# Row-by-row first projections, squares added on VectorE, a later row of factors, and sums at the end on TensorE

## The chip, the cores and the metric

The kernel runs on one core of one Trainium2 chip. A core has a matrix engine (TensorE, PE in the profile), VectorE (DVE), ScalarE (ACT), GpSimd (POOL) and SyncE (SP), which here issues the transfers. The metric is the device time of one execution in microseconds (us).

## The reference

256 tokens of width 1024 pass through two blocks in fp32. The first has attention and a mixture of 32 experts. The second is where most of the change lies: four feed-forward stages of width 2816 (ffn0 to ffn3), with a mixer with forgetting attention (fox) behind the first and one with latent attention (mla) behind the third. Each stage begins with a norm over the width.

```python
def rms_norm_2(x, g):
    xf = x.astype(jnp.float32)
    y = xf * lax.rsqrt(jnp.mean(xf * xf, axis=-1, keepdims=True) + RMS_EPS)
    return (y * g.astype(jnp.float32)).astype(x.dtype)

def swiglu(x, w_gate, w_up, w_down):
    return (jax.nn.silu(x @ w_gate) * (x @ w_up)) @ w_down
...
    for layer in range(DEPTH_2):
        h = h + 0.5 * swiglu(rms_norm_2(h, norm_ffn[layer, 0]), ffn_w_gate[layer, 0],
                             ffn_w_up[layer, 0], ffn_w_down[layer, 0])
        hn = rms_norm_2(h, norm_mix[layer])
...
            h = h + pool_fox_mixer(hn, ab_w_in[i], ab_b_forget[i], pool_w[i], pool_scale[i], ab_w_out[i])
...
            h = h + mla_mixer(hn, cos, sin, mla_w_in[i], mla_q_norm[i], mla_kv_norm[i],
...
        h = h + 0.5 * swiglu(rms_norm_2(h, norm_ffn[layer, 1]), ffn_w_gate[layer, 1],
                             ffn_w_up[layer, 1], ffn_w_down[layer, 1])
    return rms_norm_2(h, norm_final)
```

## The kernel before

The stream of activations lies transposed in SBUF (`xT`): 8 rows (`j`, or `kk` where they are contracted) of 128 channels by 256 tokens. A product keeps fp32 accuracy by splitting both sides into a high and a low half: ACT writes the high half (L195 for weights, L199 for activations), DVE subtracts it to get the low half (L196, L200), and `mm` (L149) does three matmuls for each 128 x 128 block: high by high, high by low, low by high (`ws`). Weights come from HBM through SP into `raw` tiles and are split into `hl` tiles, half a tile in each instruction.

A feed-forward stage (`ffn`) goes through 11 chunks of 256 inner columns. A chunk has three projections of 48 matmuls each: gate (into a PSUM tile `ps`), up (`psq`) and down (`psa`); down of a chunk runs behind up of the next one. `ws` first does all 8 rows for the chunk's first 128 columns (a column block), then all 8 for the second.

The norm is not applied ahead of the projections. `prep` splits `xT` with the gains alone, and squares it on the side: ACT squares two rows, `squares` adds them up (L251) and halves the sum (L253). `add_sums` sums it over channels on PE with a column of ones, `rstd` (L234, L218) and `rsqrt_of` (L219 to L229, three Newton steps of four instructions on POOL, of three on DVE) take the inverse root, and `row` spreads it over the partitions: two diagonals (`dg`, L270) by a matrix of ones on PE, copied by DVE (L273). `act` multiplies gate and up by that row of factors (L1150, L1152). So a stage's gate needs only the splits, and the factors are needed when the first chunk is activated; `aH` and `aL` are the halves of the activated chunk, which down reads.

ffn0 has its own `prep_first`, with two norms in one. Its `xT` comes from the last experts: `spread` adds the experts' results to `xT` (L982). At the end `finish` is called by the last down for each row: it squares and sums for the last norm, and `turn` transposes back to tokens by channels.

Each engine runs its instructions in the order that a scheduler of the framework gives them by its own estimates; `issue_after` only says what an instruction must stand behind, and `pins` are the last splits of a stage.

## Time and profile before

| what | value |
|---|---|
| timed runs | 1662.88, 1662.97, 1671.75 us, median 1662.97 |
| profiled execution | 1667.76 us, span 1666.0 |
| mean granted clock of TensorE | 0.977 of full |
| busy | PE 95%, weight loads 75%, DVE 56%, ACT 35%, POOL 11% |
| chain that ended last | PE 52%, DVE 5%, DMA 2%, others 1% or less each |

The span runs from the first to the last instruction; the execution's own time also counts what lies around it. By the traces' times ffn0 takes from about 690 to 885 us, fox to 988, ffn1 to 1175, ffn2 to 1368, mla to 1464, ffn3 to 1653. A busy engine in a timeline row is one that has instructions under way; the bracket at a row's end gives the idle time just before it and what ended it.

### The profile page before, as it was taken

The numbers are of one execution on the slowest core, as the hardware profiler recorded it, in microseconds if no ns is written. First come the engines' busy times: TensorE is split into PE (matmuls) and PEld (weight loads), VectorE is DVE, ScalarE is ACT, GpSimd is POOL, SyncE is SP. The second block draws the span as 40 slices with busy tenths as digits, with TensorE's granted clock in tenths as the row PEclk, the third lists the DMA queues.
The fourth block names the chain that finished last, engine by engine and source line by source line (L and its number), as shares of the span: only waits on it lengthen the run. The fifth ranks groups of instructions, "written<-read, shape, count | busy, mean of one in ns | idle before, by whom it ended". The sixth has DMA issues, their size and how long they took to land.

```text
span 1666.0 us, 26914 instructions
## 1 busy us (share of the span) xinstructions
PE 1579.0 (95%) x11231; PEld 1247.7 (75%) x11231; DVE 927.6 (56%) x1645; ACT 579.0 (35%) x885; POOL 184.0 (11%) x296
## 2 busy tenths in 40 slices
...
GB/s 379 307 207 136 264 364 366 411 421 420 421 421 421 421 421 416 351 217 205 186 181 156 123 99 193 197 200 191 164 182 195 180 155 120 71 180 200 196 108 26
DMA packets 62252, 411.11 MB, mean 247 GB/s; under 512 B 6704, under 2 KB 8752, under 8 KB 15920
## 3 DMA queue, kind: packets, MB, share of 16 engines
...
## 4 chain that ended last, share of the span: by engine, by line
PE 52%; DVE 5%; DMA 2%; POOL 1%; issue 1%; ACT 1%; DVEq 0%; SPq 0%; POOLq 0%; ACTq 0%
PE psa L149 20%; PE ps L149 17%; PE psq L149 15%; DVE x L200 1%; DVE hl L196 1%; DMA we<-in_we_dram 1%; DMA hl<-in_we_dram 1%; PE psa L448 1%; DVE xT L1141 0%; POOL rt L226 0%; POOL dg L270 0%; ACT hl L195 0%; POOL rt L227 0%; POOL ry L219 0%; POOL ry L229 0%
## 5 line engine op out<-in xcount | busy, mean ns | idle before, releaser
L195 ACT ACTIVATE hl<-raw 128x1024 fp32r<-128x1024 f32 (+1 forms) x338 | 346.6, 1060 | 414.2 <-issue 249.0
L196 DVE TENSOR_TENSOR hl<-raw,hl 128x1024 fp32r<-128x1024 f32 (+1 forms) x336 | 412.0, 1244 | 121.6 <-ACT hl L195 121.2
L149 PE MATMUL ps<-x,hl 128*128 128x256 f32 x3120 | 400.4, 287 | 14.1 <-DVE x L200 9.6
L149 PEld LDWEIGHTS ps<-x,hl 128*128 128x128 f32 x3120 | 381.1, 193 | 31.4 <-DVE x L200 12.6
L149 PE MATMUL psq<-x,hl 128*128 128x256 f32 x2160 | 259.1, 279 | 0.0
L149 PEld LDWEIGHTS psq<-x,hl 128*128 128x128 f32 x2160 | 253.7, 189 | 0.0
L149 PE MATMUL psa<-aH,hl 128*128 128x256 f32 x1408 | 251.5, 279 | 0.0
L149 PEld LDWEIGHTS psa<-aH,hl 128*128 128x128 f32 x1408 | 217.2, 188 | 0.3 <-DVE xT L1137 0.3
L149 PE MATMUL psa<-aL,hl 128*128 128x256 f32 x704 | 196.3, 279 | 0.0
L149 PEld LDWEIGHTS psa<-aL,hl 128*128 128x128 f32 x704 | 133.0, 189 | 0.0
L149 PE MATMUL psa<-hl,XT 128*64 128x512 f32 x464 | 120.8, 599 | 1.4 <-DMA hl<-in_we_dram 1.4
L1029 ACT ACTIVATE ym<-psa,gs 128x512 fp32r<-128x512 f32 x32 | 21.9, 687 | 249.0 <-PE psa L149 244.2
L149 PE MATMUL psa<-raw,XT 128*64 128x512 f32 x368 | 100.4, 599 | 1.4 <-DVEq L851 1.1
L982 DVE SCALAR_TENSOR_TENSOR xT<-ps,mod,xT 128x256 f32<-128x256 f32 x128 | 55.6, 479 | 77.9 <-PE ps L149 77.6
L251 POOL TENSOR_TENSOR sq<-sq,sq 128x512 f32<-128x512 f32 x18 | 26.8, 1491 | 464.3 <-ACT sq L244 460.7
L149 PEld LDWEIGHTS psa<-hl,XT 128*64 128x64 f32 x464 | 34.9, 137 | 55.9 <-issue 48.1
L1150 DVE TENSOR_TENSOR gr<-ps,row 128x512 f32<-128x512 f32 x44 | 30.4, 690 | 77.8 <-PE ps L149 77.8
L1030 DVE SCALAR_TENSOR_TENSOR ym<-psa,gs,ym 128x512 fp32r<-128x512 f32 x32 | 24.0, 750 | 88.4 <-ACT ym L1029 86.7
L149 PEld LDWEIGHTS ps<-GT,ym 128*128 128x128 f32 x256 | 34.2, 189 | 50.2 <-issue 38.3
L1152 DVE TENSOR_TENSOR ur<-psq,row 128x512 f32<-128x512 f32 x44 | 30.4, 690 | 74.0 <-PE psq L149 74.0
L1007 ACT ACTIVATE ac<-psa 128x512 f32<-128x512 f32 x16 | 9.6, 597 | 166.9 <-PE psa L149 140.4
L149 PE MATMUL psa<-hl,aT 128*64 128x512 f32 x240 | 63.9, 619 | 0.3 <-DVE aT L1019 0.2
...
## 6 DMA issues: line engine op xcount, KB each, us to landing
...
hl<-in_we_dram SPq DMA_DIRECT2D x88, 1024.0 KB, 18.5
...
```

Source lines behind the costliest of these rows:

```text
L149: return getattr(PE.matmul(o, l, r, start=start, stop=stop, **kw), "ins", None)
L195: A.activation(H[:, c:c + n], src[:, c:c + n], AF.Copy)
L196: (late[c > 0] if late else V).tensor_tensor(L[:, c:c + n], src[:, c:c + n], H[:, c:c + n].bitcast(F32), op=OP.subtract)
L200: v = V.scalar_tensor_tensor(L, src, scale, H.bitcast(F32), op0=OP.mult, op1=OP.subtract)
L251: E.tensor_tensor(acc[:, :w], acc[:, :w], sq[:, :w], op=OP.add)
L448: PE.transpose(bk[:, n * 128:(n + 1) * 128], P[:, n * 128:(n + 1) * 128], ident)
L982: V.scalar_tensor_tensor(xT[:, j, :], po[:, (j % 2) * T:(j % 2 + 1) * T], g2c[:, j:j + 1], xT[:, j, :], op0=OP.mult, op1=OP.add)
L1007: A.activation(ac, p1, AF.Silu)
L1029: last = A.activation(H, py[n], AF.Copy, scale=gs).ins
L1030: V.scalar_tensor_tensor(L, py[n], gs, H.bitcast(F32), op0=OP.mult, op1=OP.subtract)
L1150: V.tensor_tensor(gr, v2(pg), b2(r), op=OP.mult)
L1152: V.tensor_tensor(ur, v2(pu), b2(r), op=OP.mult)
```

## The change

1. `ws_by_k` takes the place of the first projection of each stage: for each row `kk` it goes over both column blocks, six matmuls, before the next row. It is used for chunk 0's gate, for the first projection of fox and for the first of mla.
2. The adds of squares of `prep` and `prep_first` are issued behind all eight splits, and on DVE instead of POOL.
3. In ffn1 to ffn3 the row of factors comes behind chunk 1's gate, as it did in ffn0, and chunk 0's activation with it. In ffn0 the weights of chunk 1's up wait for the end of the inverse root on DVE (`ended`) rather than for a shift (`shifted`).
4. ffn0's splits are issued in pairs between the four spreads of the last experts.
5. At the end rows 4 to 7 are squared on ACT and summed by PE alone; DVE multiplies the first half of the channels by the norm's gains straight from PSUM (before: an ACT copy and a POOL product); two of the four stores are issued by ACT.

```diff
@@ -210,7 +210,7 @@
     def small2(tag, dt=F32, w=2):
         return sm_p.tile([128, w], dt, tag=f"{tag}{w}", name=nm(tag), bufs=2 if w == 2 else 1)
-    shifted = []
+    shifted, ended = [], []
     def rsqrt_of(v, E=None, w=2):
         E = G if E is None else E
@@ -221,7 +221,7 @@
             if E is V:
                 V.scalar_tensor_tensor(t, y, -0.5, y, op0=OP.mult, op1=OP.mult)
                 V.tensor_tensor(t, t, v, op=OP.mult)
-                V.scalar_tensor_tensor(y, t, 1.5, y, op0=OP.add, op1=OP.mult)
+                ended[:] = [V.scalar_tensor_tensor(y, t, 1.5, y, op0=OP.add, op1=OP.mult).ins]
             else:
                 G.tensor_tensor(t, y, y, op=OP.mult)
                 G.tensor_tensor(t, t, v, op=OP.mult)
@@ -291,6 +291,17 @@
             mm(po, h, XH[:, k0 + kk, :], start and kk == 0, False, **kw)
             mm(po, h, XL[:, k0 + kk, :], False, False, **kw)
             i = mm(po, l, XH[:, k0 + kk, :], False, stop and kk == nk - 1, **kw)
+        return i
+
+    def ws_by_k(po, HL, XHL):
+
+        (H, L), (XH, XL) = HL, XHL
+        for kk in range(KD):
+            for m in range(2):
+                pm_, c = po[:, m * T:(m + 1) * T], slice(m * 128, m * 128 + 128)
+                mm(pm_, H[:, kk, c], XH[:, kk, :], kk + m == 0, False, skip_group_check=True)
+                mm(pm_, H[:, kk, c], XL[:, kk, :], False, False, skip_group_check=True)
+                i = mm(pm_, L[:, kk, c], XH[:, kk, :], False, kk == KD - 1, skip_group_check=True)
         return i
     def xs(po, HL, XHL, t0, c0, n, nk=KD, k0=0, start=True, stop=True):
@@ -1031,6 +1042,7 @@
         pin.append(last)
         due.extend(lambda b=b: spread(y, GT, b) for b in range(4))
+    pins, first_x = [], []
     XT, part = gather(chosen(0))
     part(0, 4)
     for p in range(NEXP // 2):
@@ -1042,7 +1054,7 @@
         W = nextW
         if part:
             XT = nextXT
-        if p in (13, NEXP // 2 - 1):
+        if p == 13:
             while due:
                 due.pop(0)()
         if p == 4:
@@ -1050,11 +1062,15 @@
         if p == 13:
             overflow()
+    first_x += [x8(F32R), x8(F32R)]
+    for b in range(4):
+        due.pop(0)()
+        for j in (2 * b, 2 * b + 1):
+            pins[:] = split(xT[:, j, :], first_x[0][:, j, :], first_x[1][:, j, :], scale=gg[:, j:j + 1])
+
     pm.close()
     pe.close()
     mark("second")
-
-    pins = []
     def after(pins):
         es = ExitStack()
@@ -1067,8 +1083,8 @@
         acc = None
         for j in range(KD):
             pins[:] = split(xT[:, j, :], XH[:, j, :], XL[:, j, :], scale=col(gname, g0 + j))
-            if j % 2:
-                acc = squares([xT[:, j - 1:j + 1, :]], acc=acc, halve=j == KD - 1)[0]
+        for j in range(1, KD, 2):
+            acc = squares([xT[:, j - 1:j + 1, :]], acc=acc, eng=V, halve=j == KD - 1)[0]
         if raw_sums:
             return (XH, XL), acc
@@ -1082,15 +1098,13 @@
         return (XH, XL), narrow
     def prep_first(pool):
-        XH, XL = x8(F32R), x8(F32R)
-        for j in range(KD):
-            pins[:] = split(xT[:, j, :], XH[:, j, :], XL[:, j, :], scale=gg[:, j:j + 1])
+        XH, XL = first_x
         w = small2("rw")
         def narrow(behind):
             bank = psa()
             v = small2("rv")
-            acc2 = squares(halves(xT), scale="fg", halve=True)[0]
+            acc2 = squares(halves(xT), scale="fg", eng=V, halve=True)[0]
             acc1 = squares(halves(xT), first=pool.tile([128, 2, T], F32, name="acc1"), eng=V, halve=True)[0]
             with tc.issue_after(behind):
                 add_sums(bank, 0, acc2)
@@ -1177,13 +1191,13 @@
                 if c == 0:
                     HLu = wf(1, c, KD)
             pg = ps()
-            last = project(HLg, pg)
-            if c == 1 and not n:
+            last = project(HLg, pg) if c else ws_by_k(pg, HLg, XHL)
+            if c == 1:
                 with tc.issue_after(last):
                     r = row(*rn)
                 act(*held, r)
             if c:
-                with tc.issue_after(shifted[-1]) if c == 1 else ExitStack():
+                with tc.issue_after(shifted[-1] if n else ended[0]) if c == 1 else ExitStack():
                     HLu = wf(1, c, KD)
             elif n:
                 rn = narrow(last)
@@ -1193,11 +1207,8 @@
                 rn = narrow(last)
             if not c:
                 acc4 += [psa() for _ in range(4)]
-                if not n:
-                    held = (c, pg, pu)
-                    continue
-                with tc.issue_after(last):
-                    r = row(*rn)
+                held = (c, pg, pu)
+                continue
             act(c, pg, pu, r)
         down(*prev.pop())
         pfs.close()
@@ -1228,7 +1239,7 @@
     u = wx.tile([128, 4, 16 + T], F32, name="uf")
     V.memset(u[:, :, 0:16], 0.0)
     pu = [ps(), psq()]
-    last = proj2(abload(0), pu[0])
+    last = ws_by_k(pu[0], abload(0), XHL)
     rt, bank = narrow(last)
     last = proj2(abload(1), pu[1])
     pf = ps()
@@ -1380,7 +1391,7 @@
     pkv, pq = psa(), ps()
     sums = psa()
-    last = proj2(miload(1), pkv)
+    last = ws_by_k(pkv, miload(1), XHL)
     kvHL, sq = latent(pkv, 1, "kvn", "ckv")
     with behind(last):
         add_sums(sums, 0, acc)
@@ -1480,29 +1491,28 @@
             for i in range(2):
                 PE.transpose(bank[2 * i + j // 4][:, (j % 4) * 128:(j % 4 + 1) * 128], xT[:, j, i * 128:(i + 1) * 128], ident)
-    def gain():
-        for i in range(2):
-            o = po_.tile([128, 512], F32, name=nm("o"))
-            A.activation(o, bank[2 * i], AF.Copy)
-            G.tensor_tensor(o, o, nfb[:, 0:512], op=OP.mult)
-            gained.append(o)
+    def gain(i):
+        o = po_.tile([128, 512], F32, name=nm("o"))
+        V.tensor_tensor(o, bank[2 * i], nfb[:, 0:512], op=OP.mult)
+        gained.append(o)
     def finish(j):
         if j == 1:
             bank.extend([ps(), ps(), psq(), psq(), psa()])
-        if j < 6:
-            acc[:] = squares([xT[:, j - 1:j + 1, :]], acc=acc[0] if acc else None, eng=V, halve=j == 5)
+        if j < 4:
+            acc[:] = squares([xT[:, j - 1:j + 1, :]], acc=acc[0] if acc else None, eng=V, halve=j == 3)
             turn(range(j - 3, j - 1) if j > 1 else [])
-        else:
-            if j == 6:
-                turn([4, 5])
-                gain()
-                add_sums(bank[4], 0, acc[0])
-            sq = po_.tile([128, 1, T], F32, name=nm("sq"))
-            A.activation(sq[:, 0], xT[:, j], AF.Square)
-            add_sums(bank[4], 0, sq, False)
-        if j == 7:
-            turn([6, 7])
+            return
+        first = j - 1 if j == 5 else j
+        if j == 5:
+            add_sums(bank[4], 0, acc[0])
+        sq = po_.tile([128, j + 1 - first, T], F32, name=nm("sq"))
+        A.activation(sq, xT[:, first:j + 1], AF.Square)
+        for q in range(j + 1 - first):
+            add_sums(bank[4], 0, sq[:, q:q + 1], False)
+        turn({5: [2, 3], 6: [4, 5], 7: [6, 7]}[j])
+        if j > 5:
+            gain(j - 6)
     ffn(3, 24, finish)
@@ -1513,8 +1523,8 @@
         A.activation(gained[i], gained[i], AF.Copy, scale=r[:, i:i + 1])
         o = po_.tile([128, 512], F32, name=nm("o"))
         V.scalar_tensor_tensor(o, bank[2 * i + 1], r[:, i:i + 1], nfb[:, 512:], op0=OP.mult, op1=OP.mult)
-        for q, t in enumerate((gained[i], o)):
-            SP.dma_start(out[i * 128:(i + 1) * 128, q * 512:(q + 1) * 512], t)
+        for q, (t, E) in enumerate(((gained[i], A), (o, SP))):
+            E.dma_start(out[i * 128:(i + 1) * 128, q * 512:(q + 1) * 512], t)
 def lay_out(i):
```

DVE at the start of ffn2, before: the end of the splits of `xT` (`x_1441` is the low half), the weight splits (`hl`), the variance (`rv`) and its shift (`ri`), up to the row of factors.

```order
L200 SCALAR_TENSOR_TENSOR x_1441_10316<-xT,cols,x_1440_10315 128x256 x4
L196 TENSOR_TENSOR hl_10505<-raw_10502,hl_10504 128x1024 x2
L196 TENSOR_TENSOR hl_10513<-raw_10510,hl_10512 128x1024 x2
L234 TENSOR_SCALAR rv_10413<-psa_10410 128x2
L218 TENSOR_SCALAR ri_10415<-rv_10413 128x2
L196 TENSOR_TENSOR hl_10570<-raw_10567,hl_10569 128x1024 x2
L273 COPY row_10490<-psa_10410 128x256
```

The same place in the changed kernel:

```order
L251 TENSOR_TENSOR sq_10333<-sq_10333,sq_10335 128x512
L196 TENSOR_TENSOR hl_10488<-raw_10485,hl_10487 128x1024
L251 TENSOR_TENSOR sq_10333<-sq_10333,sq_10338 128x512
L196 TENSOR_TENSOR hl_10488<-raw_10485,hl_10487 128x1024
L251 TENSOR_TENSOR sq_10333<-sq_10333,sq_10341 128x512
L196 TENSOR_TENSOR hl_10562<-raw_10559,hl_10561 128x1024
L253 TENSOR_TENSOR sq_10333<-sq_10333 128x256
L196 TENSOR_TENSOR hl_10562<-raw_10559,hl_10561 128x1024
L234 TENSOR_SCALAR rv_10413<-psa_10410 128x2
L218 TENSOR_SCALAR ri_10415<-rv_10413 128x2
L196 TENSOR_TENSOR hl_10570<-raw_10567,hl_10569 128x1024 x2
L196 TENSOR_TENSOR hl_10685<-raw_10682,hl_10684 128x1024 x2
```

The row just ahead of these is the last four activation splits (L200), and the row's copy comes next behind them. The three adds and the halving now stand between the weight splits, ahead of `rv`. Between `ri` and the row's copy stood two weight splits and now stand four.

PE in ffn2, before, around the diagonals: the last rows of chunk 0's up (`psq`), and chunk 1's gate (`ps`).

```order
L149 MATMUL psq_10432<-x_1440_10315,hl_10355 128x256
L149 MATMUL psq_10432<-x_1441_10316,hl_10355 128x256
L149 MATMUL psq_10432<-x_1440_10315,hl_10356 128x256
L149 MATMUL psa_10410<-dg_10485,cstt 128x128 x2
L149 MATMUL ps_10518<-x_1440_10315,hl_10512 128x256
L149 MATMUL ps_10518<-x_1441_10316,hl_10512 128x256
```

The changed kernel, around the diagonals:

```order
L149 MATMUL ps_10493<-x_1440_10315,hl_10487 128x256
L149 MATMUL ps_10493<-x_1441_10316,hl_10487 128x256
L149 MATMUL ps_10493<-x_1440_10315,hl_10488 128x256
L149 MATMUL psa_10410<-dg_10542,cstt 128x128 x2
L149 MATMUL psq_10575<-x_1440_10315,hl_10569 128x256
L149 MATMUL psq_10575<-x_1441_10316,hl_10569 128x256
```

The diagonals now stand behind chunk 1's gate and ahead of chunk 1's up; chunk 1's gate moved ahead of them.

DVE at the end of the program, before: the last evacuations of ffn3 into `xT`, the squares, and the variance of the last norm.

```order
L1141 SCALAR_TENSOR_TENSOR xT<-psa_13607,xT 128x512
L1141 SCALAR_TENSOR_TENSOR xT<-psa_13608,xT 128x512
L251 TENSOR_TENSOR sq_15454<-sq_15454,sq_15469 128x512
L1141 SCALAR_TENSOR_TENSOR xT<-psa_13609,xT 128x512
L1137 SCALAR_TENSOR_TENSOR xT<-psa_13610,xT 128x256
L251 TENSOR_TENSOR sq_15454<-sq_15454,sq_15489 128x512
L253 TENSOR_TENSOR sq_15454<-sq_15454 128x256
L1137 SCALAR_TENSOR_TENSOR xT<-psa_13610,xT 128x256
L234 TENSOR_SCALAR rv_15536<-psa_15453 128x2
```

The changed kernel, same place (`o` are the products with the gains):

```order
L1155 SCALAR_TENSOR_TENSOR xT<-psa_13607,xT 128x512
L1155 SCALAR_TENSOR_TENSOR xT<-psa_13608,xT 128x512
L251 TENSOR_TENSOR sq_15454<-sq_15454,sq_15469 128x512
L1155 SCALAR_TENSOR_TENSOR xT<-psa_13609,xT 128x512
L253 TENSOR_TENSOR sq_15454<-sq_15454 128x256
L1496 TENSOR_TENSOR o_15517<-ps_15449,x_1765_13433 128x512
L1151 SCALAR_TENSOR_TENSOR xT<-psa_13610,xT 128x256
L1496 TENSOR_TENSOR o_15534<-psq_15451,x_1765_13433 128x512
L1151 SCALAR_TENSOR_TENSOR xT<-psa_13610,xT 128x256
L234 TENSOR_SCALAR rv_15537<-psa_15453 128x2
```

One add of squares is gone, the halving stands ahead of the last two evacuations instead of between them, and two products from PSUM are new.

## Rows read from the trace of the kernel before

**Rows 1.** The page, part 1: busy us by engine (share of span).
```profile
PE 1579.0 (95%) x11231; PEld 1247.7 (75%) x11231; DVE 927.6 (56%) x1645; ACT 579.0 (35%) x885; POOL 184.0 (11%) x296
```

**Rows 2.** PE's waits, whole span: what for, us in total, times, longest.
```profile
PE ps L149 <- DVE x L200: 9.6, 13, 2.2
...
PE psa L149 <- POOL dg L270: 6.7, 5, 2.2
```

**Rows 3.** Timeline of PE, start of ffn2: start, us, instruction, count, idle before.
```profile
1175.63 1.64 PE L149 MATMUL ps<-x,hl 128*128 128x256 f32 x13
...
1180.29 5.29 PE L149 MATMUL ps<-x,hl 128*128 128x256 f32 x29 [0.80 <-DVE x L200]
1185.42 0.50 PE L149 MATMUL psa<-cstt,sq 128*128 128x1 f32 x4
...
1192.30 0.84 PE L149 MATMUL psa<-dg,cstt 128*128 128x128 f32 x4 [0.62 <-POOL dg L270]
...
1198.63 1.58 PE L149 MATMUL psq<-x,hl 128*128 128x256 f32 x12
```

**Rows 4.** Timeline of DVE, start of ffn2.
```profile
1173.03 0.48 DVE L200 SCALAR_TENSOR_TENSOR x<-xT,cols,x 128x256 fp32r<-128x256 f32 x1 [0.58 <-ACT x L199]
...
1176.47 4.63 DVE L200 SCALAR_TENSOR_TENSOR x<-xT,cols,x 128x256 fp32r<-128x256 f32 x4
1181.03 4.62 DVE L196 TENSOR_TENSOR hl<-raw,hl 128x1024 fp32r<-128x1024 f32 x4
...
1198.47 0.69 DVE L196 TENSOR_TENSOR aL<-gr,aH 128x512 fp32r<-128x512 f32 x1 [0.70 <-ACT aH L195]
```

**Rows 5.** Timeline of POOL, start of ffn2.
```profile
1175.66 4.30 POOL L251 TENSOR_TENSOR sq<-sq,sq 128x512 f32<-128x512 f32 x3 [170.70 <-ACT sq L244]
...
1186.68 1.19 POOL L226 TENSOR_TENSOR rt<-ry 128x2 f32<-128x2 f32 x1
...
1189.65 0.19 POOL L226 TENSOR_TENSOR rt<-ry 128x2 f32<-128x2 f32 x1
...
1191.88 0.72 POOL L270 TENSOR_SCALAR dg<-cstt,ry 128x128 f32<-128x128 f32 x2
```

**Rows 6.** Windows: us, busy us by engine, granted PE clock (PEclk), DMA share, GB/s.
```profile
1001.00:1013.00 12.00, 10.04 (x72) 9.78 (x72) 5.58 (x9) 3.70 (x5) 2.94 (x14) 0.86 0.59 223
1172.00:1190.00 18.00, 16.21 (x122) 15.46 (x121) 15.76 (x20) 9.70 (x17) 8.03 (x11) 0.91 0.40 148
```

**Rows 7.** Timeline of PE, start of ffn1.
```profile
988.98 2.32 PE L149 MATMUL ps<-x,hl 128*128 128x256 f32 x19
...
1012.44 1.75 PE L149 MATMUL psq<-x,hl 128*128 128x256 f32 x14
```

**Rows 8.** Timeline of PE, start of ffn3.
```profile
1464.16 0.28 PE L149 MATMUL ps<-x,hl 128*128 128x256 f32 x1
...
1487.68 2.54 PE L149 MATMUL psq<-x,hl 128*128 128x256 f32 x21
```

**Rows 9.** Timeline of PE, start of fox.
```profile
905.99 0.84 PE L149 MATMUL psa<-dg,cstt 128*128 128x128 f32 x4 [0.86 <-POOL dg L270]
```

**Rows 10.** Timeline of DVE, start of mla.
```profile
1381.54 0.17 DVE L218 TENSOR_SCALAR ri<-rv 128x4 int32<-128x4 int32 x1
```

**Rows 11.** Timeline of DVE, end of the program.
```profile
1649.82 0.69 DVE L251 TENSOR_TENSOR sq<-sq,sq 128x512 f32<-128x512 f32 x1 [0.77 <-ACT sq L244]
...
1653.09 1.37 DVE L253 TENSOR_TENSOR sq<-sq 128x256 f32<-128x256 f32 x1
...
1657.49 0.16 DVE L234 TENSOR_SCALAR rv<-psa 128x2 f32<-128x2 f32 x1 [2.70 <-PE psa L149]
```

**Rows 12.** Timeline of SP's queue, end of the program.
```profile
1660.65 1.81 SPq L1517 DMA_DIRECT2D out_dram<-o  x4
```

**Rows 13.** Chain that ended last, two projections of 48, ffn0 and ffn1.
```profile
744.79 5.65 PE ps L149 x48
...
1018.04 5.44 PE psa L149 x48
```

## The prediction

> **What bounds the kernel now.** I read the page first. TensorE (PE) is busy for 1579.0 of the 1666.0 us of the span [rows 1], so only what stops PE, or slows it, can be gained. The list of PE's waits comes next, since it says what ends those stops. Two of its entries belong to code that the change touches: 13 waits for the low half of a split activation row (`x`, L200, DVE), 9.6 us together and 2.2 the longest, and 5 waits for the factors' diagonal (`dg`, L270, POOL), 6.7 us [rows 2]. They lie at the starts of the six stages behind the experts: ffn0, fox, ffn1, ffn2, mla, ffn3.
>
> The timeline of one such start shows how it goes. In ffn2 the gate begins at 1175.63 and the matmuls of the sums follow at 1185.42 [rows 3]. That is 9.79 us for 48 matmuls, which take 5.65 at the slower of two paces that PE keeps (48 in 5.65 or in 5.44, 117.8 or 113.3 ns each [rows 13]). 4.1 us are lost. DVE and POOL show why: a split that runs alone takes 0.48, the last four take 4.63 together, 1.16 each [rows 4], while POOL adds squares (three in 4.30 [rows 5]). The old gate spends three matmuls on a split, 0.35 us, and so waits 0.80 for the next. The windows show the rest: PE's granted clock is 0.91 of full in 1172 to 1190 and 0.86 in 1001 to 1013 [rows 6], that is a stretch at 1.2 instead of 2.4 GHz that costs about 0.09 x 18 = 1.6 and 0.14 x 12 = 1.7 us. In ffn2 it comes straight behind these waits: the 29 matmuls from 1180.29 take 5.1 us until the sums, where 3.4 would do [rows 3].
>
> **The change, part by part.** I work out ffn2 and carry it to the others.
>
> *Row by row over both blocks (`ws_by_k`).* A split now feeds six matmuls, 0.71 us at 117.8 ns. Alone it costs DVE 0.48, so PE should no longer wait.
>
> *Squares on DVE.* The order puts them behind the eight splits, between splits of weights. An add alone costs 0.69 on DVE [rows 11], so three and the halving (half as wide, from that estimated at 0.4) cost 2.5. What they leave is 4 x (1.16 - 0.48) = 2.7, the time that the splits lost to POOL's adds. DVE's own total stays the same, but the activation is ready 2.7 us sooner. The sums are ready later relative to the gate: splits done at 1176.5 + 1.9 = 1178.4, then three adds, three weight splits (1.16 each [rows 4]) and the halving, 6.0 us, so 1184.4. The order has PE reach the sums 19 matmuls into the up projection, at 1175.6 + 67 x 0.1178 = 1183.5. That is a new wait of 0.9; I take 1.0.
>
> *Row held a projection longer.* Before, the diagonal's matmuls stood behind up(0) and waited for POOL until 1192.30, with up(1) at 1198.63 [rows 3]. Now gate(1) stands between: three projections of 48 (17.0), the sums 0.5, the wait 1.0 and the diagonal 0.7 (1198.63 - 1192.30 less 48 matmuls) [rows 3] give up(1) at 1175.6 + 19.2 = 1194.8, 3.8 sooner. The diagonal is due 0.7 earlier, at 1194.1. Behind it stands down(0), which needs `aL`: that ended 6.9 after the diagonal's matmuls started (1198.47 + 0.69 - 1192.30 [rows 3, 4]), while down(0) now follows their start by 0.7 + 5.65 = 6.35 and spends four matmuls, 0.5, on `aH` first: nothing, or with a weight split in the way up to 1.2; I take 0.2. ffn2: **+3.6** (2 to 4.5).
>
> *ffn1.* The gate starts at 988.98, up(1) at 1012.44 [rows 7]. Three projections at 113.3 ns (16.3), sums 0.5, a wait of 0.3 (the order has one of its adds among the splits already) and 0.7 for the diagonal put up(1) at 1006.8: 5.6 sooner, less 0.4 for `aL`, which comes later here against the faster pace. **+5.2** (3.5 to 6). *ffn3* starts at 1464.16, up(1) at 1487.68 [rows 8]: 16.3 + 0.5 + 1.0 + 0.7 = 18.5, so 1482.7, 5.0 sooner, less 0.8 (the same, and a weight split). **+4.2** (2.5 to 5).
>
> *fox* keeps its diagonal where it was, behind the first projections, at 905.99 [rows 9]. The gate ends some 4 us sooner, but the diagonal hangs on the sums, the inverse root on POOL and weight splits on DVE, all of which the adds now delay. I take a third of it, **+1.6** (0.5 to 3). *mla* waits for four factors of which the last is ready at 1381.54 [rows 10], behind weight splits on DVE that do not move: **0** (-0.5 to 2). *ffn0* has the longest of the split waits, 2.2 [rows 2], but its gate's bank is one that the spreads use, and their evacuations now stand among the splits, so it starts no sooner; what goes are the pauses behind. **+1.5** (0 to 3, the longest wait and a little more).
>
> *End.* Before, DVE's last evacuation stood behind a halving that POOL stretched to 1.37 (from 1653.09), and the variance came at 1657.49 [rows 11]. After it the chain is PE's sums, evacuated variance, ten small DVE steps, two products, the store. Now that halving is gone from there and POOL does nothing. Replaying with 0.69 for each of the two products that DVE takes over, its last evacuation starts at about 1653.3 and the variance at about 1655.2: 2.2 sooner. SP issued four stores in 1.81 [rows 12]; it now issues two, the last 0.4 to 0.9 sooner if ACT's take no longer than SP's, an issue that no row shows; I take 0.5. **+2.7** (1 to 4).
>
> The new wait for the sums may itself bring a stretch at the lower clock at one of the starts, as the waits before did (1.6 [rows 6]); with that and what the diagonal may cost in the rival below I take off 1.0. Everything else is covered: a stage that starts 4 to 6 us sooner asks for its weights sooner, and ACT and DVE, 35 and 56% busy [rows 1], have the room to split them.
>
> **Sum.** 1.5 + 1.6 + 5.2 + 3.6 + 0 + 4.2 + 2.7 - 1.0 = 17.8 us, between 8 and 26 with all bounds at their ends. The profiled execution took 1667.76 (its span 1666.0), 4.8 above the median of 1662.97; the timed runs reach from 1662.88 to 1671.75. So 1667.8 - 17.8 = **1650.0**. I don't shift it by 4.8: the likely cause of that spread is the next point, and it is drawn anew.
>
> **Rivals.**
> 1. *The pace.* ffn0 runs at 5.65 for 48, ffn1 at 5.44 [rows 13]; ffn2 is like the first and ffn3 like the second. Each is held through some 1500 matmuls, so it is worth 31 x 0.21 = 6.5 us in a stage. The clock is full in both, and the pace changes only where PE is disturbed. I found no rule in it and count each as the toss of a coin, expected no change. With three of four slow the time would be 1656.5, with all four 1663: no change that a measurement shows.
> 2. *The diagonal is late after all.* POOL's inverse root has 13 short steps; those that meet a weight split on DVE take up to 1.19 instead of 0.19 [rows 5]; in ffn2 two did. The order now has four weight splits between the shift (`ri`) and the row's copy, in ffn1 five. Two more hits put `dg` at about 1185.4 + 3.6 + 4 x 0.9 + 0.7 = 1193.3, and it is due at 1194.1: just in time. Three hits more and each FFN waits some 1.9: 1655.7. The Trainium skill (SBUF — State Buffer, "Who interferes with whom") says that DVE instructions with two SBUF inputs and GpSimd instructions that read SBUF exclude each other, the later one waiting until the first is done. By it every split behind `ri` can hold a step of POOL for its whole length, which is this rival; the trace agrees, with 1.19 against 0.19 [rows 5].
> 3. *The clock stays.* If the stretches at 1.2 GHz come anyway (another pause ahead of them), 5 of the 17.8 don't come: 1655.
> 4. *DVE becomes the bound: slower.* Each start's 2.5 us of adds stand ahead of the weight splits that PE needs next. If PE waited for all 2.5 at the six starts and each wait brought a stretch of 1.7 at the lower clock, that is 25 us: 1650 + 25 = 1675. It ends slower from about 3.6 per start on. For it: DVE is busy without a pause there. Against: DVE gets back the 2.7 it lost to POOL, and PE has a projection of 5.5 us in hand before the next weights.
>
> **How the numbers follow.** No change is what lies within 0.5% (8.3 us) of 1663, so faster is below 1654.7 and slower above 1671.3. Forecast 0.64; the diagonal 0.12, half of it mild enough to stay below 1654.7; the pace 0.12; the clock 0.06; DVE 0.06. Faster 0.64 + 0.06 = 0.70, the same 0.06 + 0.12 + 0.06 = 0.24, slower 0.06. The forecast's own range is 1641 to 1658. For 8 in 10 the upper end takes in the diagonal and most of the pace, 1662; the lower end is the sum with its gains near their upper bounds or one slow stage turned fast, 1639.
>
> **What would show it.** Right: the waits for `x` gone from the starts of ffn1, ffn2 and ffn3, up(1) 4 to 6 us sooner after the stage's first matmul, a wait of about 1 for the sums on DVE, none for `dg` in these stages, full clock in 1172 to 1190, the variance of the end some 2 sooner. Wrong: waits for `hl` or `dg` of several us there, or more stages at 5.65 than before.

## The result, and the profile after

The changed kernel has a median of 1655.95 us against 1663.81 for the kernel before on the same chip (nine executions each; two of the changed one were disturbed, at 2746 and 3949 us, and are left out of the ratio). The ratio is 0.9935, interval 0.9911 to 0.9959: faster by 0.65%. That is also the ratio of the means, 1653.97 and 1664.85; by the medians it is 0.47%. The prediction drew its line for no change at 0.5%, and this line lies inside the interval: that the kernel is faster is shown, that it is so by more than 0.5% is not. The forecast was 1650.0 in 1639 to 1662. The profiled execution took 1654.91 us, span 1653.1, 12.9 below that of before.

The page's first part and the list of PE's waits of the changed kernel, for [rows 1, 2]:

```profile
PE 1577.7 (95%) x11239; PEld 1248.5 (76%) x11239; DVE 926.0 (56%) x1670; ACT 579.2 (35%) x883; POOL 158.3 (10%) x270
```

```profile
PE psa L149 <- POOL dg L270: 5.1, 3, 3.1
PE ps L149 <- DVE xT L993: 4.0, 3, 2.5
```

The wait for `x` (L200), 9.6 us before, is not in the list any more. The one for `xT` (the spreads at ffn0's start) has grown from 1.5 to 4.0, and the halved squares now cost 0.5 in ffn2 and 0.3 in fox. The wait for the diagonal has fallen from 6.7 to 5.1, and it has moved: in ffn1 to ffn3, where it was 2.0, 0.6 and 2.2, none is left, and 3.1 of it is in ffn0.

Timeline of PE, start of ffn2, for [rows 3]:

```profile
1169.14 5.60 PE L149 MATMUL ps<-x,hl 128*128 128x256 f32 x48
1174.58 2.32 PE L149 MATMUL psq<-x,hl 128*128 128x256 f32 x19
1177.41 0.58 PE L149 MATMUL psa<-cstt,sq 128*128 128x1 f32 x4 [0.52 <-DVE sq L253]
...
1181.23 5.60 PE L149 MATMUL ps<-x,hl 128*128 128x256 f32 x48
1186.67 0.63 PE L149 MATMUL psa<-dg,cstt 128*128 128x128 f32 x4
1187.05 5.90 PE L149 MATMUL psq<-x,hl 128*128 128x256 f32 x48
```

The gate runs through in 5.44 (1169.14 to 1174.58) where its 48 matmuls took 9.79. The sums stand 19 matmuls into up(0), wait 0.52, and the diagonals follow gate(1) without a wait. up(1) starts 17.9 us after the stage's first matmul; before it was 23.0.

DVE and POOL in the same place, for [rows 4, 5]:

```profile
1169.98 1.74 DVE L200 SCALAR_TENSOR_TENSOR x<-xT,cols,x 128x256 fp32r<-128x256 f32 x4
1171.64 0.69 DVE L251 TENSOR_TENSOR sq<-sq,sq 128x512 f32<-128x512 f32 x1
...
1176.85 0.42 DVE L253 TENSOR_TENSOR sq<-sq 128x256 f32<-128x256 f32 x1
...
1178.59 2.36 DVE L196 TENSOR_TENSOR hl<-raw,hl 128x1024 fp32r<-128x1024 f32 x2
```

```profile
1178.84 1.03 POOL L219 TENSOR_SCALAR ry<-ri 128x2 int32<-128x2 int32 x1 [174.12 <-DVE ri L218]
1179.95 1.05 POOL L226 TENSOR_TENSOR rt<-ry 128x2 f32<-128x2 f32 x1
...
1182.47 1.22 POOL L228 TENSOR_SCALAR rt<-rt 128x2 f32<-128x2 f32 x1
1183.77 1.05 POOL L229 TENSOR_TENSOR ry<-ry,rt 128x2 f32<-128x2 f32 x1
...
1186.03 0.72 POOL L270 TENSOR_SCALAR dg<-cstt,ry 128x128 f32<-128x128 f32 x2
```

The last four splits take 1.74 instead of 4.63, and an add takes the 0.69 that the prediction took for it. Four of POOL's steps meet a weight split and take 1.03 to 1.22 instead of 0.19; before it was two. The second of the two diagonals ends at 1186.75, and PE starts on the first at 1186.67 without a wait: rival 2 came to just where it starts to cost.

Windows, the stretches of [rows 6], and one of ffn0 (columns as there):

```profile
1001.00:1013.00 12.00, 11.88 (x104) 11.69 (x103) 9.13 (x12) 6.33 (x8) 3.29 (x7) 1.00 0.54 182
1172.00:1190.00 18.00, 17.48 (x154) 17.31 (x153) 13.86 (x18) 8.07 (x10) 6.82 (x15) 1.00 0.66 234
714.00:739.00 25.00, 22.16 (x180) 22.11 (x181) 18.51 (x22) 10.72 (x13) 4.46 (x10) 0.93 0.60 211
```

The granted clock is 1.00 where it was 0.86 and 0.91. In ffn0 the 0.93 stands for a stretch at 1.2 GHz; before it was 1.00 there. That stretch is not in every execution of the changed kernel, as the section on ffn0 shows.

**Where the time went, stage by stage.** The table gives, in us, times between first matmuls in the traces: ffn0 from the last experts' spreads to fox; fox to ffn1; the starts of ffn1 to ffn3, from the first gate matmul to the first of down(0); mla to ffn3; the end, from ffn3's last down matmul to the end of the span. "Slow" names the FFN stages that ran at about 117.8 ns for a matmul behind their first down (0 for ffn0 and so on); the others ran at about 113.3. e1 to e12 are the runs told below; e8's starts hold 48 matmuls more.

| kernel | ffn0 | fox | ffn1 start | ffn2 start | mla | ffn3 start | end | span | slow |
|---|---|---|---|---|---|---|---|---|---|
| before | 199.09 | 103.02 | 28.89 | 28.65 | 95.93 | 28.96 | 13.45 | 1665.99 | 0, 2 |
| changed | 202.42 | 99.54 | 23.09 | 23.65 | 93.80 | 24.47 | 10.86 | 1653.13 | 0, 2, 3 |
| e1 | 200.65 | 99.57 | 23.09 | 23.87 | 93.98 | 24.61 | 10.46 | 1651.92 | 0, 1, 3 |
| e9 | 201.78 | 99.19 | 23.09 | 23.47 | 93.84 | 24.19 | 10.45 | 1643.86 | 0, 2 |
| e2 | 197.85 | 99.65 | 23.54 | 24.31 | 93.95 | 24.61 | 10.87 | 1650.76 | 1, 3 |
| e3 | 202.13 | 99.57 | 23.09 | 23.47 | 93.96 | 24.50 | 10.45 | 1640.75 | 0 |
| e4 | 202.99 | 100.73 | 23.99 | 24.42 | 95.92 | 25.61 | 10.47 | 1665.24 | all |
| e5 | 202.55 | 99.45 | 23.09 | 23.55 | 93.82 | 24.46 | 10.70 | 1658.87 | all |
| e6 | 199.96 | 99.59 | 28.32 | 27.32 | 93.89 | 30.96 | 10.72 | 1671.31 | 1, 2, 3 |
| e7 | 201.79 | 99.37 | 23.73 | 23.46 | 94.07 | 24.55 | 10.44 | 1646.35 | 0, 3 |
| e8 | 207.15 | 99.56 | 28.53 | 29.62 | 93.85 | 30.06 | 10.46 | 1658.10 | 0, 2, 3 |
| e10 | 199.16 | 99.53 | 23.09 | 23.54 | 93.85 | 24.46 | 10.47 | 1656.41 | all |
| e11 | 199.05 | 101.63 | 26.81 | 27.61 | 97.02 | 26.52 | 12.26 | 1659.06 | 0, 1 |
| e12 | 201.60 | 99.42 | 23.09 | 23.47 | 93.93 | 24.42 | 13.38 | 1641.80 | 0 |

From before to the changed kernel ffn1 to ffn3 start 5.8, 5.0 and 4.5 sooner, fox saves 3.5, mla 2.1 and the end 2.6. ffn0 loses 3.3. The rest of ffn3, from down(0) to the last down matmul, takes 167.17 instead of 159.41, most of it because the stage went at the slow pace.

How far a column moves with no edit can be read from the table too. The start of ffn1 took 23.09 in all seven executions that have the changed kernel's ffn1. The old stages repeat less well: e11 has the fox, the mla and the end of the kernel before, and takes 101.63, 97.02 and 12.26 there against 103.02, 95.93 and 13.45. Outside the FFN starts a difference of 1 to 1.5 us between two executions is therefore no finding by itself.

The theory behind the experiments: the change brings what its sum says, some 18 us, because a split now feeds six matmuls, POOL leaves the splits alone, and the diagonal has a projection more; what is missing went to ffn0's diagonal and to the pace. The rivals: the change itself makes stages slow; one of its three parts does all the work; ffn0 loses by its new start and not by its diagonal.

### The profile page after: what moved, and what is told of

Its sections match the earlier page's. It is cut to its first block, busy times and chain, and to the rows that moved or that the text cites. A ratio compares the mean times of both kernels' runs of the same rounds, so it can differ in the third digit from the quotient of the medians.

```text
span 1653.1 us, 26911 instructions
## 1 busy us (share of the span) xinstructions
PE 1577.7 (95%) x11239; PEld 1248.5 (76%) x11239; DVE 926.0 (56%) x1670; ACT 579.2 (35%) x883; POOL 158.3 (10%) x270
## 4 chain that ended last, share of the span: by engine, by line
PE 53%; DVE 4%; DMA 2%; POOL 1%; issue 1%; ACT 0%; DVEq 0%; SPq 0%; ACTq 0%; POOLq 0%
PE psa L149 20%; PE psq L149 16%; PE ps L149 16%; DMA we<-in_we_dram 1%; DVE hl L196 1%; DVE x L200 1%; DMA hl<-in_we_dram 1%; PE psa L459 1%; DVE xT L1155 0%; POOL rt L227 0%; POOL rt L228 0%; POOL ry L219 0%; DVE sq L251 0%; POOL rt L226 0%; POOL ry L229 0%
## 5 line engine op out<-in xcount | busy, mean ns | idle before, releaser
L149 PE MATMUL ps<-x,hl 128*128 128x256 f32 x3120 | 391.6, 284 | 6.1 <-ACT hl L195 2.7
L149 PEld LDWEIGHTS ps<-x,hl 128*128 128x128 f32 x3120 | 375.1, 190 | 20.8 <-issue 7.2
L1022 DVE TENSOR_TENSOR ac<-ac,psa 128x256 f32<-128x256 f32 x32 | 12.1, 417 | 91.2 <-PE psa L149 91.2
## 6 DMA issues: line engine op xcount, KB each, us to landing
hl<-in_we_dram SPq DMA_DIRECT2D x88, 1024.0 KB, 18.3
```

The source lines that it names most:

```text
L149: return getattr(PE.matmul(o, l, r, start=start, stop=stop, **kw), "ins", None)
L1022: V.tensor_tensor(ac[:, c], ac[:, c], p3[:, c], op=OP.mult)
```

## The experiments

### The pace: e1, e9, e2 and e8

**e1** and **e9** are the changed kernel once more, with no edit.

> The changed kernel once more, unchanged. If the pace of PE is set by what stands ahead of a stage (theory A), ffn0 to ffn3 run at 117.5, 113.3, 117.8 and 117.8 ns for a matmul again, as in the first profile, and the time is within 2 us of 1655. If the pace is the toss of a coin in each execution (theory B), at least one of the four is likely to differ, and the time then moves by 6.5 us for each stage.

> The changed kernel unchanged once more, timed on the same chip as the next three. If the gain is some 19 us less what the pace takes, the median is 8 to 20 us below that of before, and the stages' starts take what they took in the other profiles of it (ffn1 23.1, ffn2 23.7 to 23.9, ffn3 24.5 to 24.6 us from the first matmul to the first of down), whatever the paces are.

e1 took 1653.7 in its one execution, beside 1671.23 for the kernel before (1669.31 to 1674.79). e9 has a median of 1649.88 (1645.64 to 1657.82) beside 1668.14, ratio 0.9902 (0.9867 to 0.9938); its starts of ffn2 and ffn3 came 0.2 to 0.3 below what was expected, so the pace counts a little in them too. Chains that ended last, one projection of 48 in ffn1, ffn2 and ffn3; the changed kernel, then e1, then e9:

```profile
1016.98 5.44 PE ps L149 x48
1204.36 5.65 PE psq L149 x48
1486.58 5.65 PE psq L149 x48
```

```profile
1015.79 5.65 PE ps L149 x48
1203.55 5.44 PE ps L149 x48
1485.76 5.65 PE psq L149 x48
```

```profile
1014.26 5.44 PE ps L149 x48
1201.65 5.65 PE psq L149 x48
1483.36 5.44 PE psq L149 x48
```

One program, three patterns. e1 and e9 ran on different chips, but the chip does not set the pattern either: e9 and e10, which differ in ffn0 alone, ran on one chip, and ffn1 to ffn3 went fast, slow, fast in e9 and slow three times in e10. The pace of a stage is drawn anew in an execution and is not set by the order of instructions. e9 is the most useful profile here: its pattern is that of the profile of before, so the two can be subtracted without the pace. They differ by 22.1 us, of which 2.7 lie in the experts, ahead of the change: **19.4** remain, with what the old fox and the old end happened to take in that execution still in it.

**e2** puts idle pairs of matmuls of one column ahead of the factors' row, one pair in ffn1 and ffn2 and two in ffn3.

```diff
+    def idle_pair(p):
+        for i in range(2):
+            mm(p[:, i:i + 1], k("ones"), k("ones")[:, 0:1], True, True)
...
                 with tc.issue_after(last):
+                    for _ in range((0, 1, 1, 2)[n]):
+                        idle_pair(rn[1])
                     r = row(*rn)
```

> Two idle fp32 matmuls of one column each (a pair, 0.4 us) are put ahead of the diagonals of ffn1 (one pair), ffn2 (one pair) and ffn3 (two pairs). Theory A: each pair that PE passes without a wait turns the pace over, so ffn1 goes from 113.3 to 117.8 ns, ffn2 from 117.8 to 113.3 and ffn3 stays at 117.8; time as the changed kernel plus 1.5 us. Theory B: the pairs have nothing to do with it, and the stages are fast or slow as they happen to be.

ffn1 to ffn3 came out slow, fast, slow, but e1, which has no pairs, had just that pattern, and ffn0 turned fast in e2 with no pair in it. So the pairs don't show any hold on the pace. The median is 1652.32, ratio 0.9872 (0.9839 to 0.9905), against its own runs of before.

**e8** issues down(0) behind chunk 2's gate, so that PE has work until `aL` is there.

```diff
-            if prev:
+            if prev and c != 1:
                 down(*prev.pop())
...
+            if c == 2:
+                with tc.issue_after(last):
+                    down(*prev.pop(0))
```

> The first down of each feed-forward stage stands behind the gate of chunk 2 instead of ahead of it, so PE no longer waits there for the low half of the activated chunk (0.15 to 0.4 us in ffn1 to ffn3). If this wait is where the pace is drawn anew, a stage holds from there the pace that it has behind its diagonal: where the diagonal comes without a wait and PE runs at 113.3 behind it, the whole stage runs at 113.3. If the pace changes by itself, stages change it in the middle as well. Without a change of pace the time is 0.5 to 1 us below the changed kernel.

No pause is left at down(0). Timeline of PE in e8, ffn1:

```profile
1011.00 5.70 PE L149 MATMUL psq<-x,hl 128*128 128x256 f32 x48
1016.54 5.60 PE L149 MATMUL ps<-x,hl 128*128 128x256 f32 x48
```

From the diagonals on ffn1 held the fast pace undisturbed to its end, and ffn2 the slow one to its end. Both fit a pace that changes only at a pause; which of the two follows is not told by that. From the start of ffn1 to that of ffn2 and on to mla e8 takes 180.85 and 187.91 us, the changed kernel at the same paces 181.25 and 187.70: the gain of 0.5 to 1 us that was expected at the same pace did not come. The median is 1653.81, ratio 0.9889 (0.9833 to 0.9944).

### The parts by themselves: e6, e4, e7 and e11

**e6** undoes the later row of factors in ffn1 to ffn3 and keeps the rest.

```diff
-            if c == 1:
+            if c == 1 and not n:
                 with tc.issue_after(last):
...
-                held = (c, pg, pu)
-                continue
+                if not n:
+                    held = (c, pg, pu)
+                    continue
+                with tc.issue_after(last):
+                    r = row(*rn)
```

> In ffn1 to ffn3 the row of factors stands behind up(0) again; everything else as changed. If holding it a projection longer hides POOL's inverse root, PE waits 4 to 6 us for the diagonal in each of the three stages, and they take that much longer from their first matmul to the first of down(0), with down(0) no longer waiting for its low half. If the diagonal is ready in time anyway, the three stages stay within 1 us of 23.1, 23.65 and 24.5.

1673.1 in its one execution. The three starts lose 5.2, 3.7 and 6.5 us. The list of PE's waits of e6, and its timeline of PE in ffn2, show where:

```profile
PE psa L149 <- POOL dg L270: 15.3, 6, 4.0
```

```profile
1192.63 0.84 PE L149 MATMUL psa<-dg,cstt 128*128 128x128 f32 x4 [3.07 <-POOL dg L270]
```

Without the projection in between, PE stands 3.1, 3.1 and 4.0 us before the diagonals of ffn1, ffn2 and ffn3. A part of the loss in ffn1 and ffn3 is a stretch at the lower clock behind that wait (0.94 and 0.89 of full over the two starts, 1.00 in ffn2). Against the kernel before, e6 gains only 0.6, 1.3 and -2.0 at these starts: the sooner gate alone runs into POOL.

**e4** puts the adds of squares back on POOL.

```diff
-            acc = squares([xT[:, j - 1:j + 1, :]], acc=acc, eng=V, halve=j == KD - 1)[0]
+            acc = squares([xT[:, j - 1:j + 1, :]], acc=acc, halve=j == KD - 1)[0]
...
-            acc2 = squares(halves(xT), scale="fg", eng=V, halve=True)[0]
+            acc2 = squares(halves(xT), scale="fg", halve=True)[0]
```

> The adds of squares go back to POOL, all else as changed. If the port shared by DVE and POOL makes the splits late, the last four splits of a stage take about 1.16 us each again, PE spends only 0.7 on each, and the first projection of ffn2 takes 7 to 8 us instead of 5.5; from its first matmul to the first of down ffn2 takes 1 to 3 us longer than 23.65, and so do ffn1 (23.1) and ffn3 (24.5). If the row by row order alone took the waits away, these three stay within 0.5 us.

1667.03 in its one execution, with all four stages slow. Against the changed kernel the starts lose 0.9, 0.8 and 1.1, fox 1.2 and mla 2.1. DVE in e4, the last splits of ffn2:

```profile
1178.45 4.65 DVE L200 SCALAR_TENSOR_TENSOR x<-xT,cols,x 128x256 fp32r<-128x256 f32 x4
```

1.16 each again, beside POOL's adds. So the adds are what stretches the splits, as the prediction read it; and with six matmuls to a split even the stretched ones cost little in an FFN. The waits for them are 0.5 at most, ffn2's gate takes 6.2 where 7 to 8 was expected, and a part of the three losses is the slow pace (ffn2's gate(1) takes 5.79 against 5.44). With the adds on POOL mla takes 95.92, as before the change (95.93): by these executions its gain is this part.

**e7** undoes `ws_by_k` alone, in the FFNs, fox and mla.

```diff
-            last = project(HLg, pg) if c else ws_by_k(pg, HLg, XHL)
+            last = project(HLg, pg)
...
-    last = ws_by_k(pu[0], abload(0), XHL)
+    last = proj2(abload(0), pu[0])
...
-    last = ws_by_k(pkv, miload(1), XHL)
+    last = proj2(miload(1), pkv)
```

> The first projections go block by block again in all stages (in ffn0 too); the squares stay on DVE behind the splits. If DVE's splits alone (0.48 us against 0.35 us of PE for three matmuls) still make PE wait, and the waits were worth a part of the gain, the first projection of ffn2 takes 0.3 to 1 us longer; the three stages ffn1 to ffn3 lose 0.3 to 1 us each. If the squares' place was all, the stages stay within 0.3 us. If the row by row order was all, they lose 2.5 to 4 us each.

1648.14 in its one execution. It loses 0.64 in ffn1, 0.3 in mla, and -0.2 to 0.1 in ffn2, ffn3 and fox. Once POOL adds nothing beside it a split takes 0.42 to 0.48, and three matmuls, 0.35, nearly cover it. So the order row by row, which the prediction put first, is worth little as long as the adds are on DVE, and the adds on DVE little as long as the order is row by row: either of the two feeds the gate. e11, which has neither, loses 2.0 to 4.0 at each start against the changed kernel.

**e11** is the kernel before with nothing but the later row.

```diff
-            if c == 1 and not n:
+            if c == 1:
                 with tc.issue_after(last):
...
-                if not n:
-                    held = (c, pg, pu)
-                    continue
-                with tc.issue_after(last):
-                    r = row(*rn)
+                held = (c, pg, pu)
+                continue
```

> The kernel before with one part of the change, the row of factors held a projection longer in ffn1 to ffn3. If that part is the gain by itself, the three stages take 23 to 25 us from their first matmul to the first of down, and the median is 12 to 15 us below before. If it only frees what the other parts have not used up already (PE keeps its waits for x and its stretches at half clock, and loses only the wait for the diagonal), replayed with the rows of before the stages take about 25.3, 28.0 and 26.7 us, 6 us together, and fox, mla and the end stay as before.

The starts save 2.1, 1.0 and 2.4 us against before. The waits for `x` stay; PE in ffn1 of e11:

```profile
991.50 4.83 PE L149 MATMUL ps<-x,hl 128*128 128x256 f32 x26 [0.81 <-DVE x L200]
```

Its median is 1652.25 (1646.31 to 1667.37), ratio 0.9916 (0.9886 to 0.9947), which is more than the 5.5 us of the three starts are worth (0.3%). The profile gives no ground for the rest; the pace may hold it, which is not shown. So the starts fit the second expectation, and the time, 15.9 below before, is nearer the 12 to 15 of the first. By time, then, e11 cannot be told from the whole change on the same chip (e9, 0.9867 to 0.9938): what follows rests on the traces of the starts alone.

So in ffn1 to ffn3 the row alone saves 5.5, the other parts without it nothing (e6: 0.6 + 1.3 - 2.0 = -0.1), all together 15.3. The gate must be fed, and the diagonal must not be due before POOL has it; either alone leaves PE waiting at the other.

### ffn0: e5, e3 and e10

ffn0 lost 3.3 us where +1.5 was expected. PE and POOL there, changed kernel:

```profile
694.53 7.33 PE L149 MATMUL ps<-x,hl 128*128 128x256 f32 x48 [2.54 <-DVE xT L993]
...
716.84 0.84 PE L149 MATMUL psa<-dg,cstt 128*128 128x128 f32 x4 [3.10 <-POOL dg L270]
717.43 7.32 PE L149 MATMUL psq<-x,hl 128*128 128x256 f32 x48
```

```profile
713.16 1.04 POOL L228 TENSOR_SCALAR rt<-rt 128x2 f32<-128x2 f32 x1
714.28 1.05 POOL L229 TENSOR_TENSOR ry<-ry,rt 128x2 f32<-128x2 f32 x1
...
716.24 0.19 POOL L229 TENSOR_TENSOR ry<-ry,rt 128x2 f32<-128x2 f32 x1
716.41 0.72 POOL L270 TENSOR_SCALAR dg<-cstt,ry 128x128 f32<-128x128 f32 x2
```

The kernel before, at its diagonals:

```profile
719.78 0.84 PE L149 MATMUL psa<-dg,cstt 128*128 128x128 f32 x4 [0.97 <-POOL dg L270]
```

Before, the diagonals stood 40 matmuls into chunk 1's up and waited 0.97; now they stand ahead of it, due 40 matmuls (4.7 us) sooner. Their factors come from DVE at 713.00, but POOL is busy with the inverse root of the other norm until 716.43. In the order of before POOL made them after six of that root's thirteen steps, at 719.36; now they stand behind all thirteen. No run undoes the new order (the waiting for `ended`) by itself.

Behind the wait up(1) takes 7.3 us instead of 5.65, at the lower clock. The wait does not always bring that. PE in e1, which has no edit, and e1's window:

```profile
717.05 0.84 PE L149 MATMUL psa<-dg,cstt 128*128 128x128 f32 x4 [3.10 <-POOL dg L270]
717.65 5.70 PE L149 MATMUL psq<-x,hl 128*128 128x256 f32 x48
```

```profile
714.00:739.00 25.00, 21.95 (x192) 21.90 (x193) 19.03 (x22) 10.93 (x13) 4.67 (x10) 1.00 0.61 212
```

The same wait of 3.10 stands there with the clock at 1.00 behind it, and so it does in e9, e7 and e12. In 714 to 739 it is 0.93 in the changed kernel, e2, e3 and e4, and 0.86 in e5, e6 and e8, that is some 1.75 and 3.5 us lost (25 x 0.07 and 25 x 0.14). So times of ffn0 are to be compared at the same clock.

**e5** undoes the pairs of splits between the spreads.

```diff
-        if p == 13:
+        if p in (13, NEXP // 2 - 1):
             while due:
...
-    first_x += [x8(F32R), x8(F32R)]
-    for b in range(4):
-        due.pop(0)()
-        for j in (2 * b, 2 * b + 1):
-            pins[:] = split(xT[:, j, :], first_x[0][:, j, :], first_x[1][:, j, :], scale=gg[:, j:j + 1])
...
-        XH, XL = first_x
+        XH, XL = x8(F32R), x8(F32R)
+        for j in range(KD):
+            pins[:] = split(xT[:, j, :], XH[:, j, :], XL[:, j, :], scale=gg[:, j:j + 1])
```

> ffn0 starts as before the change (all four spreads, then the eight splits); everything else as changed. If the splits between the spreads hold back the spreads' evacuations (the gate's long run of matmuls began 8.6 us after the spreads' first matmul, against 6.8 before the change), it begins 6.8 us after it again and the start of fox comes 200.5 to 201 us after the spreads' first matmul, at the pace of 117.5 ns in ffn0, against 202.4. If the new start is worth something, it comes later than 202.4.

The run of the gate starts 6.87 us after the spreads' first matmul instead of 8.61, but ffn0 stays at 202.55, above the 200.5 to 201 expected, with 3.2 before the diagonals. That does not clear the new start: e5 reaches up(0) 14.7 us and the diagonals 30.1 us after the spreads' first matmul, the changed kernel 15.8 and 30.9 (the kernel before reaches up(0) at 15.1), and what e5 gained by then went behind them, at the lower clock (0.86 against 0.93). The old start is worth about 1 us here, and the wait is there with either. (1660.66 in its one execution, all four stages slow.)

**e3** has POOL make the diagonals ahead of the other inverse root.

```diff
+            with tc.issue_after(dgs[-1]):
+                y2 = rsqrt_of(w)
+            r2 = row(y2, psq()[:, :T])
-            r2 = row(rsqrt_of(w), psq()[:, :T])
```

> In ffn0 POOL makes the diagonal of the stage's factors ahead of the inverse root of the other norm, which it did first in the changed kernel. If the 3.1 us wait for this diagonal, and the stretch at half clock behind it (1.7 us), are what ffn0 lost, the time from the spreads' first matmul to the start of fox falls from 202.4 to 198 to 199.5 us. If ffn0 lost it by the splits between the spreads (the gate's start at 694.5 rather than 693.7, and half clock there), it stays above 201.

The wait falls only to 1.72, and ffn0 stays at 202.13: the expected 198 to 199.5 was missed. POOL in e3 shows why the wait is still there:

```profile
714.31 2.69 POOL L270 TENSOR_SCALAR dg<-cstt,ry 128x128 f32<-128x128 f32 x2 [21.53 <-DVE ry L224]
```

The two diagonals now meet two weight splits on DVE and take 2.69 instead of 0.72. That the stage gains nothing has another reason. The wait is 1.4 shorter, but the gate, ahead of the edit, ran longer at the lower clock (8.54 us for its 48 matmuls, 7.33 in the changed kernel), and the stretch behind the diagonals came here too. (1642.57 in its one execution, one stage slow.)

**e10** has DVE make ffn0's diagonals, so that neither POOL's queue nor its reads stand in the way.

```diff
-                    r = row(*rn)
+                    r = row(*rn, None if n else V)
```

> As the changed kernel, but ffn0's diagonal is made by DVE, behind its own inverse root, instead of POOL. Two such instructions take 0.28 us each on DVE elsewhere in the trace. If ffn0 loses what it loses because the diagonal, now asked for earlier, waits in POOL's queue and for the port, PE's wait for it falls from 3.1 us to below 0.7, and the start of fox comes 197 to 199.5 us after the spreads' first matmul at 117.5 ns (about 5 less at 113.3), against 200.7 to 202.5; the median falls by 2.5 to 4 us against the changed kernel on the same chip. If ffn0 loses it elsewhere, both stay.

DVE and PE in ffn0 of e10:

```profile
714.86 0.49 DVE L268 TENSOR_SCALAR dg<-cstt,ry 128x128 f32<-128x128 f32 x2
```

```profile
715.34 0.61 PE L149 MATMUL psa<-dg,cstt 128*128 128x128 f32 x4
715.70 5.25 PE L149 MATMUL psq<-x,hl 128*128 128x256 f32 x44
```

The two diagonals take 0.49, and PE no longer waits for them: the order now has four matmuls of up(1) first, which wait 0.21 for their weights. ffn0 takes 199.16, as expected. The clock stays full behind the diagonals, as in e1, e7, e9 and e12, so these are the runs to compare it with: from the spreads to down(0) e10 takes 34.3 us and they take 36.9 to 37.4; in the whole of ffn0 it is 1.5 to 2.6 less. So the cause of the wait is the diagonals on POOL: the queue ahead of them and the splits beside them, and lifting the queue alone was not enough (e3). e10's median of 1646.32 (1644.83 to 1658.19), ratio 0.9873 (0.9842 to 0.9905), is the lowest of the kernels with several executions and below the kernel before. From e9, the changed kernel beside it, its time can't be told, since the intervals overlap; that it gains on it rests on the stage alone.

### The end: e12

**e12** undoes the change at the end of the program (squares of rows 4 and 5 on DVE, the copy on ACT and the product on POOL, all four stores by SP).

```diff
-        V.tensor_tensor(o, bank[2 * i], nfb[:, 0:512], op=OP.mult)
+            A.activation(o, bank[2 * i], AF.Copy)
+            G.tensor_tensor(o, o, nfb[:, 0:512], op=OP.mult)
...
-        if j < 4:
+        if j < 6:
...
-        for q, (t, E) in enumerate(((gained[i], A), (o, SP))):
-            E.dma_start(out[i * 128:(i + 1) * 128, q * 512:(q + 1) * 512], t)
+        for q, t in enumerate((gained[i], o)):
+            SP.dma_start(out[i * 128:(i + 1) * 128, q * 512:(q + 1) * 512], t)
```

> As the changed kernel with the end of before. If the end's chain is what the prediction replayed, the time from the first down of ffn3 to the last instruction is 2 to 3 us more than the changed kernel's 177.6 to 178.0 (at 117.8 ns; 171.7 at 113.3), with the variance read 2 us later behind the last evacuation. If the products and the second queue cost what they save, it stays within 0.5 us.

The end takes 13.38 instead of 10.45 (e9). Together with the downs ahead of it, it is 1.3 us longer, between the two expectations. DVE there, the changed kernel first, then e12, for [rows 11]:

```profile
1642.59 0.42 DVE L1151 SCALAR_TENSOR_TENSOR xT<-psa,xT 128x256 f32<-128x256 f32 x1 [1.62 <-PE psa L149]
1644.57 0.16 DVE L234 TENSOR_SCALAR rv<-psa 128x2 f32<-128x2 f32 x1 [1.55 <-PE psa L149]
```

```profile
1630.27 0.41 DVE L1151 SCALAR_TENSOR_TENSOR xT<-psa,xT 128x256 f32<-128x256 f32 x1
1633.30 0.16 DVE L234 TENSOR_SCALAR rv<-psa 128x2 f32<-128x2 f32 x1 [2.62 <-PE psa L149]
```

The last evacuation starts as soon as PE is done, where in e12 it stands behind the stretched halving, and the variance comes 1.98 behind it instead of 3.03. But this second part is not the change's own. e11, which has the old end as well, takes 1.90 there, with a granted clock of 0.84 over the 4 us from the last evacuation's start, where it was 0.56 in e12. The sums of PE in e12, then in e11:

```profile
1630.49 1.60 PE L149 MATMUL psa<-cstt,sq 128*128 128x1 f32 x8 [1.57 <-DVE sq L253]
```

```profile
1648.88 1.02 PE L149 MATMUL psa<-cstt,sq 128*128 128x1 f32 x8 [1.58 <-DVE sq L253]
```

So the old end takes 12.26 or 13.4 by the clock that it meets, and the new one 10.4 to 10.9. And ffn3 from down(0) to its last down takes 1.7 less in e12 (159.57 against 161.24 in e9, both fast): the sums and transposes that left the end now stand among the downs. Net 1.3 remain against e12, and about nothing against e11. (1643.98 in its one execution, one stage slow.)

The stores bring nothing. DMA issues at the end of the changed kernel, then of e12 (the last number is us from issue to landing), for [rows 12]:

```profile
out_dram<-o ACTq DMA_DIRECT2D x2, 256.0 KB, 3.0
out_dram<-o SPq DMA_DIRECT2D x2, 256.0 KB, 3.1
```

```profile
out_dram<-o SPq DMA_DIRECT2D x4, 256.0 KB, 2.4
```

Two issues on each side take 0.94 and 0.98 instead of 1.81 on one, but the stores then take 0.6 to 0.7 longer to land. From the variance to the end of the span it is 8.56 in the changed kernel and 8.50 in both kernels with the old end. The Trainium skill (DMA: Bandwidth & Descriptors, "Issuing engines are not separate DMA queues") says that transfers issued by several engines share the same DMA engines and that only issue time is saved. These rows agree that issue time is saved, and here the landing gave it back.

## Why the prediction was right, and where it was off

The time fell in the range and on the side that was forecast, 6 us above the forecast. The forecast took its 17.8 off the profiled 1667.76, so it was 13.0 below the median of 1662.97; measured were 7.9 by the medians and 10.9 by the means. Its sum against the profile of the changed kernel and against e9, which has the pace pattern of before (us saved; "start" and the rest of the stage together):

| term | forecast | changed | e9 |
|---|---|---|---|
| ffn0 | +1.5 | -3.3 | -2.7 |
| fox | +1.6 | +3.5 | +3.8 |
| ffn1 | +5.2 | +5.4 | +5.4 |
| ffn2 | +3.6 | +4.9 | +4.9 |
| mla | 0 | +2.1 | +2.1 |
| ffn3 start | +4.2 | +4.5 | +4.8 |
| down(0) of ffn3 to the last down | 0 | -7.8 | -1.8 |
| end | +2.7 | +2.6 | +3.0 |
| clock and diagonal | -1.0 | in ffn0 | in ffn0 |
| ahead of the change | 0 | +1.0 | +2.7 |
| sum | 17.8 | 12.9 | 22.1 |

That the totals of 12.9 and 22.1 lie on either side of 17.8 is in part luck: ffn0 and the downs fell short by 4 to 5 and by 2, fox, mla and ffn2 brought about 5 more than forecast, and the pace and the clock of an execution move the whole by more than any of these.

- **The three FFN starts** were the core of the argument, and 13.0 forecast became 14.8 to 15.1. The waits for `x` went, the sums wait 0.52 (1.0 forecast), `dg` is just in time, the clock is full. What feeds the gate is not the six matmuls for a split alone, as the prediction had it, but either them or the adds' place (e4, e7). ffn2 was put too low by 1.3: its start ran at the fast pace (three projections in 16.3 instead of 17.0), and the wait for the sums was half of that taken.
- **Four hits** on POOL in ffn2, two more than before, are rival 2's first half, and it priced them about rightly (0.8 to spare by its sum; measured 0.08 late, at no wait that shows). e6 is that rival in full, with 3.07 where the row is not held.
- **fox and mla** were mis-sized. "The adds now delay" the row in fox, and mla's splits "do not move": both steps counted DVE's new adds and not what POOL's adds had cost the splits in front of the shift. In mla the shift `ri` now starts 12.2 us after the stage's first matmul (1369.03 - 1356.84), before 13.3 [rows 10], with three adds and the halving ahead of it. In fox the diagonals' matmuls start 16.4 after the stage's first one, before 20.0 [rows 9]; POOL's two diagonals take 0.72 there now, before 2.71. By e4 the adds' place is 2.1 in mla, all of its gain, and 1.2 of fox's 3.5; of the rest of fox 1.4 is what e11 saves there with no edit, at a full clock where the kernel before had 0.93.
- **ffn0** is the step that failed. The prediction looked at the gate's start and its pauses, and not at the diagonals, which the order had moved 40 matmuls forward. e10 shows the price, 2.6 to 3.1 us by down(0). The 1.0 taken off for a late diagonal and a new stretch of low clock belonged here, at three times its size. And the +1.5 was not there to begin with: without the wait, in e10, ffn0 takes 199.16, as before the change (199.09). The pauses in the gate did go, but the gate starts later behind the spread splits and up(0) comes at 15.8 us instead of 15.1.
- **The end** gained as forecast on its own stretch, but some 1.2 of that is the low clock that the old end met in the kernel before and not in e11, the work moved into the downs cost 1.7 to 1.8, which the sum did not count, and the 0.5 for the stores did not come.
- **The pace**, rival 1, explains the rest of the profile: three slow stages where before had two, one stage costs 5.9 us from ffn3's down(0) to its last down alone (167.17 against 161.24). For three slow stages the rival gave 1656.5; the median is 1655.95. That the median lies where it does because of the pace is not shown, since only profiled executions show it; the repeat on another chip came out 18.3 below its own kernel before, this one 7.9.

What stays open is what decides the pace, what decides whether a wait is followed by the lower clock (in ffn0 the same 3.1 us was and was not), and why the kernel before, with a median of 1663.81 here, took 1668 to 1671 beside the experiments.
